# Value projection of one attention layer: two groups of eight heads with 512 columns per product, instead of four groups of four heads with 256

## The chip, the cores and the metric

The kernel runs on one core of a Trainium2 chip. The metric is the device time of one execution in microseconds (us). TensorE (PE) multiplies, VectorE (DVE) and ScalarE (ACT) do the elementwise work, GpSimd (POOL) does some elementwise work and issues a few transfers, and SyncE (SP) issues most transfers.

## The reference, cut to what matters

A trunk of two layers over 1024 positions and 1024 channels. Layer 0 has dilated attention and pooling side by side, layer 1 a gated unit and a state-space layer (S5); each layer ends with cross-attention. The change touches the attention of layer 0 alone:

```
hn = rms_norm(x, norm_ab[i])
z = hn @ w_in_ab[i]
q, k, v, g_a, v_b, g_b = jnp.split(z, [...], axis=-1)     # q, k, v: 1024 columns, 16 heads of 64
a_out = dilated_attention(q, k, v).reshape(b, s, A_WIDTH) * jax.nn.silu(g_a)
```

Each of three patterns (window, dilation) is a banded softmax over keys at a stride; the three are mixed by their denominators.

## The kernel before, in words

Every product of f32 matrices is made of three passes over rounded halves (high times high, high times low, low times high), so a product with 1024 input channels is 8 x 3 = 24 matmuls into one PSUM tile. The weights come in tiles of 128x1024 in a fixed list (`plan`). `get` loads tiles ahead through the SP queue (`wst`), ACT copies the rounded high half (`wh`, L177) and DVE subtracts for the low half (`wl`, L178); `s.deep` says how many are loaded and split ahead.

The stage of interest (`ab_main` with `ab_side`) handles the 16 heads as eight pairs, `pr` = 0 to 7. For each pair, `ab_pair` projects q, k and the gate (`ga`): three weights times two halves of the positions, six tiles of 24 matmuls with 512 columns, line L203 to L205. The values of several heads are projected ahead of them by `ab_v`: for each of eight blocks of 128 positions (`tt`) a tile with the positions on the partitions, which ACT scales (`vt`, L464) and writes to a scratch tensor in HBM; `ab_pair` reads its two heads' columns from there (`V`, `Vp`).

The attention itself is a second generator, `ab_side`. It works in 64 blocks, numbered here i = 8 x pair + b. A step of it is: the transposes of block i-1 (`turn`, PE L547 and L551), the scores of block i (`front`, PE L519), the products of block i-1 with the values (`mix`, PE L566), and every fourth step the products of the strided keys (`last`, PE L577). Between `front` of a block and its transposes lies the softmax for two heads: DVE adds the mask (L526) and takes the maximum (L527), ACT exponentiates (L528), DVE inverts the sum and scales (L529, L530). After the transposes ACT copies a part out of PSUM (`PT`, L553), which `mix` reads, and DVE another (`PTr`, L556). "Turn i" below means the transposes of block i on PE.

`drive` interleaves the two: whenever the main generator yields 1, the side generator earns 0.55 of a step. `mm3` with 8 terms yields once in its middle, and `ab_pair` once after each tile. `in_order` fixes PE's order to the order of the program text, so between two attention steps stand as many products as the yields let through. A pair may start only when the attention is at most two pairs behind:

```
            while s.attn_done < pr - 2:
                yield 2
```

A yield of 2 runs one step of the side at once, with no product between. From its eighth step on, each attention step also takes a piece of the S5 layer's preparation (`s5_prep`, mostly small POOL operations, L904 to L909, on tiles `s5z` and `trig`) and places it behind the step's own instructions.

Of the kernel before, what the change touches and what calls it, by code (L numbers as in the profile page):

```python
# [10 lines left out]
AF = mybir.ActivationFunctionType  # L11
# [19 lines left out]
def layout(i):  # L31
    f = {n: np.asarray(v) for n, v in i.items()}
    c = np.ascontiguousarray
    o = {}
    o["xT"] = c(f["x"][0].T.reshape(8, 128, 1024))
    o["memT"] = c(f["mem"][0].T.reshape(8, 128, 256).transpose(1, 0, 2).reshape(128, 2048))
    cols = [f["norm_ab"][0], f["norm_cd"][0], f["norm_x"][0], f["norm_x"][1], f["mem_norm"], f["final_norm"],
            f["pool_scale"][0], f["sgu_ln_g"][0], f["sgu_ln_b"][0]]
    o["gains"] = c(np.stack(cols).reshape(72, 128).T)
    o["w_kv"] = c(np.stack([_chunks(f["w_xkv"][l]) for l in range(2)]))  # L40
    o["w_q"] = c(np.stack([_chunks(f["w_xq"][l].T) for l in range(2)]))
    o["w_o"] = c(f["w_xo"].reshape(2, 4, 2, 128, 2, 512).transpose(0, 1, 4, 3, 2, 5).reshape(2, 8, 128, 1024))
    w = f["w_in_ab"][0]
    o["w_ab"] = c(_chunks(np.concatenate([w[:, :2048], w[:, 3072:]], axis=1)))
    o["w_v"] = c(w[:, 2048:3072].reshape(2, 4, 128, 4, 256).transpose(3, 0, 2, 1, 4).reshape(8, 128, 1024))
    o["pool_w"] = c(f["pool_w"][0].reshape(4, 2, 128, 256).transpose(0, 2, 1, 3).reshape(4, 128, 512))
    o["w_out_ab"] = c(f["w_out_ab"][0].reshape(2, 8, 128, 8, 128).transpose(3, 0, 2, 1, 4).reshape(16, 128, 1024))
    w = f["w_in_cd"][0]
    o["w_cd"] = c(_chunks(np.concatenate([w[:, :1024], w[:, 2048:]], axis=1)))
    o["w_vc"] = c(w[:, 1024:2048].reshape(4, 2, 128, 2, 512).transpose(3, 0, 2, 1, 4).reshape(8, 128, 1024))  # L50
    o["w_glu"] = c(np.concatenate([_chunks(f["glu_w1"][0]), _chunks(f["glu_w2"][0])], axis=2))
    o["w_out_cd"] = c(f["w_out_cd"][0].reshape(2, 6, 128, 8, 128).transpose(3, 0, 2, 1, 4).reshape(16, 128, 768))
    o["sgu_wT"] = c(f["sgu_w"][0].transpose(2, 0, 1).reshape(128, 512))
    o["sgu_b"] = c(np.broadcast_to(f["sgu_b"][0].reshape(1, 512), (128, 512)))

    def both(t):
        rep = np.broadcast_to(t.T[None], (2, 64, 32)).reshape(128, 32)
        pair = t.reshape(16, 2, 64).transpose(1, 2, 0).reshape(128, 16)
        return np.concatenate([rep, pair], axis=1)

    dt = np.broadcast_to(f["s5_log_dt"][0][:, None], (32, 64))
    o["s5_p"] = c(np.concatenate([both(f["s5_a_re"][0]), both(f["s5_a_im"][0]), both(dt)], axis=1))
    st = []
    for n in ("s5_b_re", "s5_b_im"):
        st.append(f[n][0].transpose(1, 0, 2).reshape(64, 512))
    for n in ("s5_c_re", "s5_c_im"):
        st.append(f[n][0].transpose(2, 0, 1).reshape(64, 512))
    st = np.stack(st, axis=1).reshape(64, 2048)
    o["s5_bc"] = c(np.broadcast_to(st[None], (2, 64, 2048)).reshape(128, 2048))
    d = f["s5_d"][0].reshape(32, 16).T  # L70
    o["s5_d"] = c(np.broadcast_to(d[None], (8, 16, 32)).reshape(128, 32))

    p = np.arange(128)
    t = 4 * (p % 32) + p // 32
    j1 = np.concatenate([t, t + 128])
    dist = 128 + t[:, None] - j1[None, :]
    m1 = np.where((dist >= 0) & (dist <= 128), 0.0, NEG)

    def m23(q, k):
        dd = q[:, None] - k[None, :]  # L80
        n = (dd >= 0) * ((dd <= 128).astype(int) + (dd % 4 == 0))
        return np.where(n == 0, NEG, np.where(n == 2, math.log(2.0), 0.0))

    cst = [m23(p % 32, np.arange(32)), m1[:, 128:], m23(p % 32 + 224, np.arange(256)), m1]
    cst.append(np.eye(128, 240))
    cst.append(np.broadcast_to(1.0 / np.arange(1, 17)[None], (128, 16)))
    cst.append(((p[:, None] >= 112) & (p[:, None] % 16 == np.arange(16)[None])).astype(float))
    o["cst"] = c(np.concatenate(cst, axis=1).astype(np.float32))
    return o
# [6 lines left out]
class Prog:  # L96
    def __init__(s, nc, tc, a, pool, psum, dram):
        s.nc, s.tc, s.a, s.pool, s.psum, s.dram = nc, tc, a, pool, psum, dram
        s.plan, s.index, s.W, s.st = [], {}, {}, {}
        s.n_load = s.n_split = s.pos = 0  # L100
# [81 lines left out]
    def get(s, key):  # L182
# [7 lines left out]
        s.pos = i + 1  # L190
        return s.W[i]

# [256 lines left out]
            s.flush()  # L449
        s.last = p  # L450

    def ab_v(s, qd):
        nc = s.nc
        vd = s.dt(f"v{qd}", [1024, 256])
        s.vd[qd] = vd
        keys = [("v", 2 * qd), ("v", 2 * qd + 1)]
        W = [s.get(k) for k in keys]
        for tt in range(8):
            p = s.pm()
            h, o = tt // 4, 128 * (tt % 4)  # L460
            yield from s.mm3(p[:, :256], [((s.xg[k, h][0][:, o:o + 128], s.xg[k, h][1][:, o:o + 128]),
                                           tuple(w[:, 256 * (k % 4):256 * (k % 4) + 256] for w in W[k // 4])) for k in range(8)])
            t = s.u("vt")
            nc.scalar.activation(t[:, :256], p[:, :256], AF.Copy, scale=s.Rt[:, tt:tt + 1])  # L464
            nc.scalar.dma_start(vd[128 * tt:128 * tt + 128, :], t[:, :256])
        for k in keys:
            s.free(k)

    def ab_pair(s, pr):
        nc = s.nc  # L470
        q, kk, ga = (s.b(n) for n in ("q", "kk", "ga"))
        V, Vp = s.b("V"), s.b("Vp")
        vd, c0 = s.vd[pr // 2], 128 * (pr % 2)
        for r in range(4):
            nc.sync.dma_start(V[32 * r:32 * r + 32, :].rearrange("i (t c) -> i t c", t=8),
                              vd[:, c0:c0 + 128].rearrange("(t i r) c -> r i t c", i=32, r=4)[r])
        for hh in range(2):
            nc.sync.dma_start(Vp[:, 512 * hh:512 * hh + 512].rearrange("p (r c) -> p r c", r=4),
                                vd[512 * hh:512 * hh + 512, c0:c0 + 128].rearrange("(p r) c -> p r c", r=4))
        held, R8 = {}, s.R8  # L480
        for h in range(2):
            yield from s.proj(("ab", pr), h, held)
            s.anchor = nc.vector.tensor_tensor(q[:, 512 * h:512 * h + 512].rearrange("p (b r i) -> p b r i", b=4, r=4),
                                               s.last.rearrange("p (b i r) -> p b r i", b=4, r=4),
                                               R8[h].rearrange("p (b i r) -> p b r i", b=4, r=4), op=ALU.mult)
            yield 1
        for h in range(2):
            yield from s.proj(("ab", 8 + pr), h, held)
            s.anchor = nc.vector.tensor_tensor(kk[:, 512 * h:512 * h + 512].rearrange("p (b r i) -> p b r i", b=4, r=4),
                                               s.last.rearrange("p (b i r) -> p b r i", b=4, r=4),  # L490
                                               s.R[h].rearrange("p (b i r) -> p b r i", b=4, r=4), op=ALU.mult)
            yield 1
        for h in range(2):
            yield from s.proj(("ab", 16 + pr), h, held)
            s.anchor = nc.vector.tensor_tensor(ga[:, 512 * h:512 * h + 512], s.last, s.R[h], op=ALU.mult)
            if h == 1:
                nc.scalar.activation(ga, ga, AF.Silu)
            yield 1
        s.pair[pr] = (q, kk, ga, V, Vp)
# [148 lines left out]
    def ab_main(s):  # L648
        s.R8 = [s.u("R8") for _ in range(2)]
        for h in range(2):  # L650
            s.nc.gpsimd.tensor_scalar(s.R8[h], s.R[h], 0.125, None, op0=ALU.mult)
        s.vd, s.pair, s.gd, s.attn_done = {}, {}, {}, -1
        for pr in range(8):
            if pr % 2 == 0:
                yield from s.ab_v(pr // 2)
            while s.attn_done < pr - 2:
                yield 2
            yield from s.ab_pair(pr)
        for gi in range(4):
            if s.attn_done == 7:  # L660
                s.mtags = ("mm", "s", "o")
            yield from s.ab_pool(gi)
# [768 lines left out]
def plan(s):  # L1431
    a = s.a
# [8 lines left out]
        for d in range(8):  # L1441
            s.add(("o", l, d), a["w_o"][l, d])
    for pr in range(8):
        if pr % 2 == 0:
            s.add(("v", pr), a["w_v"][pr])
            s.add(("v", pr + 1), a["w_v"][pr + 1])
        for j in (0, 8, 16):
            s.add(("ab", j + pr), a["w_ab"][j + pr])
    for gi in range(4):
# [83 lines left out]
```

## Time and profile before

| | |
|---|---|
| time, median of 3 runs | 2112.68 us (2112.36 to 2113.53) |
| profiled execution | 2116.89 us, of which 2115.2 us span |
| mean granted TensorE clock | 0.989 |
| PE busy | 2061.8 us (97%) |
| DVE, ACT, POOL busy | 1144.8, 767.5, 534.8 us |

The span runs from the first to the last instruction of the program; busy times are unions of an engine's instructions. PE is the engine that nearly always works; the other three wait for it, or it for them in short places. The stage of the attention runs from 200 to about 850 us of the span.

### The profile page before, as it was taken

How to read it: one execution, taken by the hardware profiler on the slowest of the kernel's cores; microseconds unless marked ns; L12 is line 12 of the kernel's file. 1: busy time of each engine (PE TensorE's matmuls, PEld its weight loads, DVE VectorE, ACT ScalarE, POOL GpSimd, SP SyncE). 2: the span in 40 equal slices, each digit the busy share in tenths (PEclk: the TensorE clock that was granted, in tenths of full speed). 3: DMA queues.
4: the chain of work that ended last, by engine and by line, in shares of the span. 5: the costliest groups of instructions: out<-in, count | busy, mean ns of one | idle time of the engine just before them, and what ended most of it. 6: DMA issues, size and time to landing. Idle time of an engine off the chain costs nothing.

```text
span 2115.2 us, 33157 instructions
## 1 busy us (share of the span) xinstructions
PE 2061.8 (97%) x12974; PEld 1729.7 (82%) x12974; DVE 1144.8 (54%) x2067; ACT 767.5 (36%) x1442; POOL 534.8 (25%) x802
## 2 busy tenths in 40 slices
PE   8999999899999988999999999999999999999998
PEld 8999888687787766888888888888888887888887
DVE  6664266566655775456453655444653334555554
ACT  7765243333333333114332444212221122443453
POOL 4332017722333244122111003221221100220013
PEclk9999999999999999999999999999999999999999
DMA  7888212103114112116464125532331134642142
GB/s 293 301 292 281 73 33 86 56 24 119 51 65 114 62 51 86 56 66 222 146 208 164 46 101 183 166 119 70 116 113 70 58 102 157 202 165 74 51 169 80
DMA packets 131468, 258.63 MB, mean 122 GB/s; under 512 B 13040, under 2 KB 63344, under 8 KB 131312
## 3 DMA queue, kind: packets, MB, share of 16 engines
q1 hardware_dynamic: 86608, 189.39, 26.8%
q0 software_dynamic: 13440, 43.53, 5.6%
q10 hardware_dynamic: 31264, 23.60, 3.6%
q8 instruction: 102, 1.67, 0.3%
q14 instruction: 54, 0.44, 0.1%
HBM read 193.02 MB, written 63.44 MB: 121 GB/s over the span
## 4 chain that ended last, share of the span: by engine, by line
PE 87%; DVE 5%; POOL 3%; ACT 2%; issue 2%; DMA 1%; SPq 0%; DVEq 0%; ACTq 0%; POOLq 0%
PE ps_mm L203 13%; PE ps_mm L204 13%; PE ps_mm L205 13%; PE ps_s L204 5%; PE ps_s L205 5%; PE ps_s L203 5%; PE ps_o L205 4%; PE ps_o L204 4%; PE ps_o L203 4%; PE ps_s L519 2%; PE ps_o L566 1%; PE ps_mm L1311 1%; PE ps_mm L1309 1%; PE ps_mm L1310 1%; PE ps_t L547 1%
## 5 line engine op out<-in xcount | busy, mean ns | idle before, releaser
L178 DVE TENSOR_TENSOR wl<-wst,wh 128x1024 fp32r<-128x1024 f32 (+1 forms) x263 | 345.8, 1329 | 128.3 <-ACT wh L177 123.3
L203 PE MATMUL ps_mm<-xg,wh 128*128 128x512 f32 x880 | 350.1, 398 | 1.3 <-DVE ug L1338 1.0
L204 PE MATMUL ps_mm<-xg,wh 128*128 128x512 f32 x880 | 343.7, 391 | 0.0
L205 PE MATMUL ps_mm<-xg,wl 128*128 128x512 f32 x880 | 343.3, 390 | 0.0
L177 ACT ACTIVATE wh<-wst 128x1024 fp32r<-128x1024 f32 (+1 forms) x263 | 262.0, 1016 | 113.4 <-PE ps_mm L204 84.5
L203 PEld LDWEIGHTS ps_mm<-xg,wh 128*128 128x128 f32 x880 | 165.4, 188 | 43.3 <-issue 8.3
L205 PEld LDWEIGHTS ps_mm<-xg,wl 128*128 128x128 f32 x880 | 165.3, 188 | 34.9
L204 PEld LDWEIGHTS ps_mm<-xg,wh 128*128 128x128 f32 x880 | 165.6, 188 | 32.4 <-issue 0.2
L240 POOL TENSOR_TENSOR acc<-acc,sq 128x512 f32<-128x512 f32 (+1 forms) x81 | 102.5, 1266 | 215.0 <-ACT sq L236 202.5
L223 ACT ACTIVATE xg<-x,gains 128x512 fp32r<-128x512 f32 x64 | 46.2, 722 | 246.3 <-DVE x L753 187.4
L528 ACT ACTIVATE P<-P,mx 128x320 f32<-128x320 f32 (+7 forms) x128 | 77.9, 610 | 136.6 <-DVE mx L527 132.9
L553 ACT ACTIVATE PT<-ps_t 128x256 f32<-128x256 f32 (+1 forms) x128 | 45.3, 369 | 174.2 <-PE ps_t L551 172.7
L592 POOL DMA_DIRECT2D gab<-G x32 | 18.1, 567 | 244.2 <-DVE G L580 126.9
L530 DVE TENSOR_SCALAR P<-P,den 128x320 f32<-128x320 f32 (+7 forms) x128 | 77.2, 604 | 4.4
L556 DVE COPY PTr<-ps_t 128x128 f32<-128x128 f32 (+2 forms) x192 | 46.0, 281 | 55.8 <-ACT PT L553 52.8
L224 DVE SCALAR_TENSOR_TENSOR xg<-x,gains,xg 128x512 fp32r<-128x512 f32 x64 | 52.1, 815 | 42.1 <-ACT xg L223 40.8
L203 PE MATMUL ps_mm<-wh,xg 128*128 128x256 f32 x256 | 73.9, 289 | 0.0
L205 PE MATMUL ps_mm<-wh,xg 128*128 128x256 f32 x256 | 72.5, 283 | 0.0
L204 PE MATMUL ps_mm<-wl,xg 128*128 128x256 f32 x256 | 72.4, 283 | 0.0
L1338 DVE TENSOR_TENSOR ug<-ps_mm,R 128x512 f32<-128x512 f32 x32 | 22.1, 689 | 90.4 <-PE ps_mm L205 90.3
L526 DVE TENSOR_TENSOR P<-ps_s,cst 128x320 f32<-128x320 f32 (+7 forms) x128 | 65.0, 549 | 8.3 <-PE ps_s L519 6.4
L547 PE MATMUL ps_t<-cst,P 128*128 128x128 f32 x240 | 47.5, 281 | 21.0 <-DVE den L529 15.0
(423 smaller groups left out, 5115.1 us busy)
## 6 DMA issues: line engine op xcount, KB each, us to landing
wst<-w_ab SPq DMA_DIRECT2D x40, 512.0 KB, 3.4
wst<-w_out_ab SPq DMA_DIRECT2D x32, 512.0 KB, 4.3
wst<-vsc SPq DMA_DIRECT2D x32, 512.0 KB, 4.0
wst<-w_kv SPq DMA_DIRECT2D x31, 512.0 KB, 5.9
wst<-w_cd SPq DMA_DIRECT2D x24, 512.0 KB, 3.4
wst<-w_out_cd SPq DMA_DIRECT2D x32, 384.0 KB, 3.3
wst<-w_q SPq DMA_DIRECT2D x16, 512.0 KB, 8.1
msc<-mo ACTq DMA_DIRECT2D x32, 256.0 KB, 6.2
```

Of the source, the lines that this page charges most:

```text
L177: s.last_hi = s.nc.scalar.activation(H[:, :w], t[:, :w], AF.Copy)
L178: s.nc.vector.tensor_tensor(L[:, :w], t[:, :w], H[:, :w], op=ALU.subtract)
L203: s.nc.tensor.matmul(ps, lhsT=lh, rhs=rh, start=(i == 0), stop=False)
L204: s.nc.tensor.matmul(ps, lhsT=lh, rhs=rl, start=False, stop=False)
L205: s.nc.tensor.matmul(ps, lhsT=ll, rhs=rh, start=False, stop=(i == n - 1))
L223: nc.scalar.activation(H, x, AF.Copy, scale=g)
L224: nc.vector.scalar_tensor_tensor(L, x, g, H, op0=ALU.mult, op1=ALU.subtract)
L240: nc.gpsimd.tensor_tensor(st["acc"][:, :n], st["acc"][:, :n], q[:, :n], op=ALU.add)
L526: nc.vector.tensor_tensor(t[:, :n], p[e][:, :n], s.cst[:, m0:m0 + n], op=ALU.add)
L528: j = nc.scalar.activation(t[:, :n], t[:, :n], AF.Exp, bias=mx, accum_out=den)
L530: nc.vector.tensor_scalar(t[:, :n], t[:, :n], den, None, op0=ALU.mult)
L547: nc.tensor.transpose(pt[:, 128 * j:128 * j + 128], t[:, n2 + 128 * j:n2 + 128 * j + 128], s.ident)
```

## The change

The 1024 value columns are projected in two groups (`g`) instead of four (`qd`). A product has 512 columns instead of 256, and a group reads four weight tiles, which are taken one by one as the first block of positions needs them and given back one by one in the last. Within a group, five tiles instead of three are split ahead. `ab_v` yields twice per block of positions instead of once. `ab_main` calls it before pairs 0 and 4 instead of before pairs 0, 2, 4 and 6, and the list of weights follows.

```
-    def ab_v(s, qd):
-        nc = s.nc
-        vd = s.dt(f"v{qd}", [1024, 256])
-        s.vd[qd] = vd
-        keys = [("v", 2 * qd), ("v", 2 * qd + 1)]
-        W = [s.get(k) for k in keys]
+    def ab_v(s, g):
+
+        nc = s.nc
+        s.vd[g] = vd = s.dt(f"v{g}", [1024, 512])
+        keys = [("v", 4 * g + j) for j in range(4)]
+        W, deep = {}, s.deep
+        s.deep = (1, 5)
         for tt in range(8):
             p = s.pm()
             h, o = tt // 4, 128 * (tt % 4)
-            yield from s.mm3(p[:, :256], [((s.xg[k, h][0][:, o:o + 128], s.xg[k, h][1][:, o:o + 128]),
-                                           tuple(w[:, 256 * (k % 4):256 * (k % 4) + 256] for w in W[k // 4])) for k in range(8)])
+            for k in range(8):
+                if k // 2 not in W:
+                    W[k // 2] = s.get(keys[k // 2])
+                H, L = W[k // 2]
+                c0 = 512 * (k % 2)
...
+                nc.tensor.matmul(p, lhsT=lh, rhs=H[:, c0:c0 + 512], start=(k == 0), stop=False)
+                nc.tensor.matmul(p, lhsT=lh, rhs=L[:, c0:c0 + 512], start=False, stop=False)
+                nc.tensor.matmul(p, lhsT=ll, rhs=H[:, c0:c0 + 512], start=False, stop=(k == 7))
+                if tt == 7 and k % 2 == 1:
+                    if k == 7:
+                        s.deep = deep
+                    s.free(keys[k // 2])
+                if k == 3:
+                    yield 1
             t = s.u("vt")
-            nc.scalar.activation(t[:, :256], p[:, :256], AF.Copy, scale=s.Rt[:, tt:tt + 1])
-            nc.scalar.dma_start(vd[128 * tt:128 * tt + 128, :], t[:, :256])
-        for k in keys:
-            s.free(k)
+            nc.scalar.activation(t, p, AF.Copy, scale=s.Rt[:, tt:tt + 1])
+            nc.scalar.dma_start(vd[128 * tt:128 * tt + 128, :], t)
+            yield 1
...
         for pr in range(8):
-            if pr % 2 == 0:
-                yield from s.ab_v(pr // 2)
+            if pr % 4 == 0:
+                yield from s.ab_v(pr // 4)
             while s.attn_done < pr - 2:
                 yield 2
             yield from s.ab_pair(pr)
```

What PE does between two attention steps changes with it. First the place at the start of pair 2, from turn 5 on. The names are those of the section above; `ps_o<-PT,V` is `mix`, `ps_t<-cst,P` the transposes, `ps_s<-kk,q` a `front`. Before, `mix` of block 5 was followed by 48 products of the second value group, of which the first three stand here:

```order
L547 MATMUL ps_t<-cst,P 128x128 x2
L551 MATMUL ps_t<-cst,P 128x128 x2
L519 MATMUL ps_s<-kk,q 32x256 x8
L519 MATMUL ps_s<-kk,q 32x224 x8
L566 MATMUL ps_o<-PT,V 64x4x32 x4
L203 MATMUL ps_mm<-wh,xg_648 128x256
L204 MATMUL ps_mm<-wl,xg_648 128x256
L205 MATMUL ps_mm<-wh,xg_648 128x256
```

Now the same `mix` is followed by turn 6, `front` of block 7, `mix` of block 6 and turn 7 (the lines are 14 higher in the new text):

```order
L533 MATMUL ps_s<-kk,q 32x256 x8
L533 MATMUL ps_s<-kk,q 32x224 x8
L580 MATMUL ps_o<-PT,V 64x4x32 x4
L561 MATMUL ps_t<-cst,P 128x128 x2
L565 MATMUL ps_t<-cst,P 128x128 x2
L561 MATMUL ps_t<-cst,P 128x128 x2
L565 MATMUL ps_t<-cst,P 128x128 x2
L533 MATMUL ps_s<-kk,q 32x256 x16
L580 MATMUL ps_o<-PT,V 64x4x32 x4
L561 MATMUL ps_t<-cst,P 128x128 x2
L565 MATMUL ps_t<-cst,P 128x128 x2
```

The products between `front` and turn of a block, counted through PE's whole order, change like this (24 products are one tile; a number with "v" is of the value projection, with 256 columns before and 512 now):

| turn | 5 | 6 | 7 | 8 | 14 | 15 | 16 | 31 | 32 | 39 | 40 | 46 | 47 | 48 |
|---|---|---|---|---|---|---|---|---|---|---|---|---|---|---|
| before | 12+12v | 48v | 48v | 48v | 24 | 24 | 0 | 72 | 0 | 12+12v | 48v | 24 | 72 | 0 |
| now | 12 | 0 | 0 | 0 | 12 | 12 | 0 | 144+24v | 0 | 12 | 0 | 12 | 12 | 0 |

Turns 23 to 31 run beside the second value group (before: 23 to 28 beside the third of four, half as wide). Turns 9, 10 and 41 to 45 have 24 products of the pairs and none of the value projection, of which they had some before. Turns 49 to 63 are as before.

Second, DVE's order at the end of pair 2. `s5z` is the S5 preparation, whose RECIPROCAL waits for POOL. Before, it stood behind block 15's softmax and ahead of block 16's:

```order
L529 RECIPROCAL den<-den 128x1
L530 TENSOR_SCALAR P<-P,den 128x512
L495 TENSOR_TENSOR ga<-ps_mm,R_81 128x512
L556 COPY PTr<-ps_t 128x4x32 x2
L1028 RECIPROCAL s5z<-s5z 128x48
L526 TENSOR_TENSOR P<-ps_s,cst 128x160 x2
```

Now it stands inside block 15's softmax (128x512), ahead of its scaling:

```order
L540 TENSOR_TENSOR P<-ps_s,cst 128x512 x2
L541 TENSOR_REDUCE mx<-P 128x1 x2
L1042 RECIPROCAL s5z<-s5z 128x48
L543 RECIPROCAL den<-den 128x1
L544 TENSOR_SCALAR P<-P,den 128x512
L509 TENSOR_TENSOR ga<-ps_mm,R_81 128x512
```

On POOL, 113 instructions now stand between the transfer of block 7's result (`gab<-G`) and the one that this RECIPROCAL waits for, instead of 120; the other seven have moved ahead of the transfer.

## Rows read from the trace of the kernel before

**Rows 1.** The chain that ended last, from the page: share of the span by engine.

```profile
PE 87%; DVE 5%; POOL 3%; ACT 2%; issue 2%; DMA 1%; SPq 0%; DVEq 0%; ACTq 0%; POOLq 0%
```

**Rows 2.** Windows: stretch, length, PE, PEld, DVE, ACT, POOL busy, PEclk, DMA.

```profile
223.00:985.00 762.00, 731.24 (x6038) 592.15 (x6037) 452.58 (x951) 244.59 (x526) 274.13 (x519) 0.98 0.22 71
```

**Rows 3.** Lines L203 and L519: count, shortest/median/longest ns, first and last start.

```profile
L203 PE MATMUL ps_mm<-xg,wh x880: 387/389/796, 223.4 to 1736.1; 128*128 128x512 f32 x176
...
L203 PE MATMUL ps_mm<-wh,xg x256: 277/283/388, 200.3 to 633.8; 128*128 128x256 f32 x128
...
L519 PE MATMUL ps_s<-kk,q x2048: 189/376/633, 261.6 to 817.6; 64*32 64x256 f32 x94, 64*32 64x128 f32 x23, 64*32 64x64 f32 x12, 64*32 64x160 f32 x12
```

**Rows 4.** Timeline of PE, turn 10 to turn 11: start, duration, instruction.

```profile
343.76 0.38 PE L547 MATMUL ps_t<-cst,P 128*128 128x128 f32 x2
...
345.90 0.50 PE L203 MATMUL ps_mm<-xg,wh 128*128 128x512 f32 x1
...
351.48 0.38 PE L547 MATMUL ps_t<-cst,P 128*128 128x128 f32 x2
```

**Rows 5.** Timeline of PE, turn 22; [idle before <- what ended it].

```profile
445.83 0.41 PE L547 MATMUL ps_t<-cst,P 128*128 128x128 f32 x2 [0.63 <-DVE P L530]
```

**Rows 6.** Timeline of all engines, turn 15 to turn 16.

```profile
385.61 0.38 PE L547 MATMUL ps_t<-cst,P 128*128 128x128 f32 x2
...
386.65 1.28 ACT L497 ACT_TABLE_LOAD   x1
...
387.94 1.06 ACT L497 ACTIVATE ga<-ga 128x1024 f32<-128x1024 f32 x1
...
389.33 0.65 PE L566 MATMUL ps_o<-PT,V 128*64 128x128 f32 x6 [1.88 <-ACT PT L553]
...
392.01 0.45 DVE L1028 RECIPROCAL s5z<-s5z 128x48 f32<-128x48 f32 x1 [4.86 <-POOL s5z L909]
...
395.69 0.45 PE L547 MATMUL ps_t<-cst,P 128*128 128x128 f32 x1 [5.71 <-DVE den L529]
```

**Rows 7.** Timeline of DVE and ACT, softmax of block 6.

```profile
304.62 0.98 DVE L556 COPY PTr<-ps_t 128x128 f32<-128x128 f32 x4 [1.60 <-ACT PT L553]
...
305.67 1.22 DVE L526 TENSOR_TENSOR P<-ps_s,cst 128x480 f32<-128x480 f32 x2
...
306.81 1.20 DVE L527 TENSOR_REDUCE mx<-P 128x1 f32<-128x480 f32 x2
...
307.53 1.28 ACT L528 ACT_TABLE_LOAD   x1 [2.44 <-DVE mx L527]
...
308.82 0.70 ACT L528 ACTIVATE P<-P,mx 128x480 f32<-128x480 f32 x1
...
309.84 0.47 DVE L530 TENSOR_SCALAR P<-P,den 128x480 f32<-128x480 f32 x1
```

**Rows 8.** Timeline of PE, turns 8, 32 and 48 and the product behind each.

```profile
328.35 0.27 PE L547 MATMUL ps_t<-cst,P 128*128 128x128 f32 x1
...
331.69 0.39 PE L203 MATMUL ps_mm<-wh,xg 128*128 128x256 f32 x1
...
536.78 0.65 PE L566 MATMUL ps_o<-PT,V 128*64 128x128 f32 x6 [1.88 <-ACT PT L553]
539.24 0.45 PE L547 MATMUL ps_t<-cst,P 128*128 128x128 f32 x1 [1.81 <-DVE den L529]
...
545.51 0.50 PE L203 MATMUL ps_mm<-xg,wh 128*128 128x512 f32 x1
...
685.00 0.30 PE L547 MATMUL ps_t<-cst,P 128*128 128x128 f32 x1 [1.81 <-DVE den L529]
...
690.09 0.50 PE L203 MATMUL ps_mm<-xg,wh 128*128 128x512 f32 x1
```

**Rows 9.** Windows, the step that begins with turn 32; columns as in group 2.

```profile
540.00:546.00 6.00, 6.00 (x72) 4.82 (x71) 3.64 (x11) 1.69 (x6) 0.00 (x0) 0.55 0.01 3
```

**Rows 10.** Timeline of POOL: the transfer of block 7's result.

```profile
333.25 0.64 POOL L592 DMA_DIRECT2D gab<-G  x1 [3.76 <-DVE den L529]
```

More of the change, by code (lines that the diff above doesn't have):

```diff
@@ L44, in layout @@
     o["w_ab"] = c(_chunks(np.concatenate([w[:, :2048], w[:, 3072:]], axis=1)))
-    o["w_v"] = c(w[:, 2048:3072].reshape(2, 4, 128, 4, 256).transpose(3, 0, 2, 1, 4).reshape(8, 128, 1024))
+    o["w_v"] = c(w[:, 2048:3072].reshape(4, 2, 128, 2, 512).transpose(3, 0, 2, 1, 4).reshape(8, 128, 1024))
     o["pool_w"] = c(f["pool_w"][0].reshape(4, 2, 128, 256).transpose(0, 2, 1, 3).reshape(4, 128, 512))
@@ L460, in ab_v @@
             h, o = tt // 4, 128 * (tt % 4)
-            yield from s.mm3(p[:, :256], [((s.xg[k, h][0][:, o:o + 128], s.xg[k, h][1][:, o:o + 128]),
-                                           tuple(w[:, 256 * (k % 4):256 * (k % 4) + 256] for w in W[k // 4])) for k in range(8)])
+            for k in range(8):
[3 more added lines that the diff above has]
+                c0 = 512 * (k % 2)
+                xh, xl = s.xg[k, h]
+                lh, ll = xh[:, o:o + 128], xl[:, o:o + 128]
+                nc.tensor.matmul(p, lhsT=lh, rhs=H[:, c0:c0 + 512], start=(k == 0), stop=False)
[7 more added lines that the diff above has]
+                    yield 1
             t = s.u("vt")
-            nc.scalar.activation(t[:, :256], p[:, :256], AF.Copy, scale=s.Rt[:, tt:tt + 1])
-            nc.scalar.dma_start(vd[128 * tt:128 * tt + 128, :], t[:, :256])
-        for k in keys:
-            s.free(k)
+            nc.scalar.activation(t, p, AF.Copy, scale=s.Rt[:, tt:tt + 1])
+            nc.scalar.dma_start(vd[128 * tt:128 * tt + 128, :], t)
+            yield 1
     def ab_pair(s, pr):
@@ L472, in ab_pair @@
         V, Vp = s.b("V"), s.b("Vp")
-        vd, c0 = s.vd[pr // 2], 128 * (pr % 2)
+        vd, c0 = s.vd[pr // 4], 128 * (pr % 4)
         for r in range(4):
@@ L1443, in plan @@
     for pr in range(8):
-        if pr % 2 == 0:
-            s.add(("v", pr), a["w_v"][pr])
-            s.add(("v", pr + 1), a["w_v"][pr + 1])
+        if pr % 4 == 0:
+            for j in range(4):
+                s.add(("v", pr + j), a["w_v"][pr + j])
         for j in (0, 8, 16):
```

## The prediction

> **What bounds the kernel now.** I read the chain that ended last first: PE holds 87% of it [rows 1], so a change is worth what it takes from PE's work, less the new holes that it opens in it. The change lies in the attention stage, so I then read the windows: PE works 731.2 of 762 us there [rows 2]. The holes, 31 us, are few, and what ends them is the softmax (DVE, ACT) or the copy behind the transposes (ACT), seen in the timeline. An attention step is a loop over four engines, and PE can go on only because products stand between `front` of a block and its turn. With 24 of them, turn 11 follows turn 10 after 7.72 us without a wait; the step's own PE work is 345.90 - 343.76 = 2.1 us of it [rows 4]. With 12, turn 22 waits 0.63 us [rows 5]. With none, PE stands: 1.88 us for the copy and 1.81 us for the softmax around turn 32 [rows 8], 1.88 and 5.71 us around turn 16 [rows 6]. So cover is what to count, and the order of instructions gives it exactly.
>
> **What is removed.** The first value group begins at 200.3 us and the first projection behind it at 223.4, so 192 products of 256 columns take 23.1 us, 0.120 us each; the 168 products of 512 columns from 223.4 to the first `front` at 261.6 take 0.227 us each [rows 3]. 768 x 0.120 = 92.4 us become 384 x 0.227 = 87.3 us: **-5.1 us**, and it all lies on PE's path. The Trainium skill (TensorE: Matmul & The Clock Gate, Back-to-back issue gap) puts a warm product at N / 2.4 GHz plus 2.5 ns, which is 109 and 216 ns; by it the gain would be 1.0 us, and the sum below 4 us higher. The evictions (`vt`) and their transfers halve in number; ACT is not what PE waits for there, so I cost them at nothing, covered by the products of the next block of positions.
>
> **What is moved: cover.** The products of two value groups used to stand beside turns 5 to 10 and 39 to 44. They now stand ahead of pair 0, where no attention runs, and beside turns 23 to 31, which were covered anyway. As pair 2 and later pair 3, 6 and 7 must not start before the attention has caught up, side steps are now run in a row.
>
> *Turns 6, 7, 8* lose 48 products each.
> - Turn 6 comes just after pair 1's gate. As in turn 15 to 16, ACT loads a table and runs the SiLU between the two copies out of PSUM, so that `mix` goes on only 389.33 - 385.61 = 3.72 us after the turn's start [rows 6]. Behind it stand two `PTr` copies, two mask additions, the first maximum, a second table load that itself waits for the maximum, the exponential and the scaling; in block 6 that was 304.62 to 310.31, 5.69 us with four copies, so 5.2 with two [rows 7]. Together 8.9 us, against own PE work of about 2.5 (2.1 in rows 4 for a small block; these are larger, an estimate): 6.4 us lost. From below: the 3.4 of turn 7; from above: turn 16's 7.6 plus the clock, 10.5 [rows 6].
> - Turn 7 has no table load. With 12 products the hole is 0.63 us [rows 5]; without these 2.73 us more: 3.4.
> - Turn 8 is the small first block of the next pair, like turn 32: 1.88 + 1.81 = 3.7 [rows 8].
> - The clock: from turn 8 to the next product PE took 3.34 us where nothing had stopped it, and 6.27 us from turn 32, behind two idle stretches [rows 8], with a granted clock of 0.55 in that window, that is mostly 1.2 instead of 2.4 GHz [rows 9]. I add the 2.9 us once.
>
> Together **+16.4** (10.2 to 34).
>
> The Trainium skill (ScalarE: Activation LUTs, What ACT_TABLE_LOAD costs) adds a drain of 1.38 us to each load of 1.28. Here the SiLU starts 1.29 us after its load [rows 6] and the exponential 1.29 us after its own [rows 7], so I see no drain; with it, turns 6 and 40 would cost 2.8 us more each.
>
> *Turns 14 and 15* keep 12 of 24 products: 2 x 0.63 = **+1.3** (0 to 3.8, the second by 1.88 each).
>
> *Turns 15 and 16 and POOL.* DVE's RECIPROCAL of the S5 preparation waited 4.86 us for POOL already [rows 6], and held turn 16. It now stands in front of block 15's scaling, so it holds turn 15. POOL's time to it hangs on the transfer of block 7's result, which came 333.25 - 328.35 = 4.9 us after turn 8 [rows 8, 10]; with the slow clock 7.8. From there to the RECIPROCAL at 392.01 were 58.8 us for 120 instructions, now 113: 55.3. So turn 15 can start at turn 8 plus 63.1, plus the RECIPROCALs and the scaling, 64.3. PE itself would be there after 6.3 + 5.5 to turn 9, 4 x 7.72 + 1.0 (one `last`) to turn 13 and 2 x 5.6 for the half-covered ones, 55 us; such steps were sometimes a little longer, so I take a stall of 8 instead of 9.5. Turn 16 then costs what turn 32 did, 3.7 + 2.9 = 6.6, instead of 7.6 + 2.9 = 10.5. Net **+4.1** (-3.9 if POOL is in time, +6).
>
> *Turns 39, 46, 47* are left with 12 products: 3 x 0.63 = 1.9. *Turn 40* has none: 6.6 like turn 32. *Turn 48* had none before either, but 72 products just ahead; it cost 3.7 + (5.09 - 3.34 = 1.75) [rows 8] and now 6.6: 1.2. Together **+9.7** (3.7 to 17).
>
> Turn 31 gets 168 products in a row; attention is starved there, PE is not. The weights of the value groups are split among other work: for the first group in the prologue, ahead of 200 us, for the second at turns 18 to 22, so I cost this at nothing; the cover is one attention step per tile.
>
> **Sum**: -5.1 + 16.4 + 1.3 + 4.1 + 9.7 = +26.4 us. On the profiled execution's 2116.9 us that is 2143.3; this execution was 4.2 us above the median of the runs, 2112.7, so the time to expect is **2139 us**. The low ends add to -5.1 + 10.2 + 0 - 3.9 + 3.7 = +4.9 (2118), the high ones to some +56 (2169).
>
> **Rivals.**
> 1. *The chain shrinks to nothing* (other side). In steps that run in a row, DVE and ACT have no q, k or gate to evict and few weights to split, so softmax might follow at once; then only the 5.1 us are left: 2107.6 us. It decides at turn 6: the gain wins if all new holes stay under 5.1 us. Against it: around turn 32 nothing else ran on DVE or ACT than the step itself and the table loads, and PE still stood 3.7 us [rows 8]. Chance 0.05.
> 2. *POOL is in time* (turn 15). If it needs under 47 us for its 113 instructions, turn 15 waits for the softmax alone, and -3.9 takes the place of +4.1: +18, 2131; with turn 6 at 3.4 as well, 2128. For it: the 58.8 us may hold waits of POOL for other engines, which then go. Against it: DVE waited 4.86 us for POOL with more time given [rows 6]. Chance 0.22.
> 3. *A table load costs twice.* If ACT must run empty ahead of each load, its 1.28 us [rows 6, 7] count double where nothing covers them, at turns 6 and 40 with two loads each: 5.1 us more, 2144. Against it the 1.29 us above. The Trainium skill's drain, named above, is this case. Chance 0.03.
> 4. *Weights come late* in the second group: ACT's rounding of a tile stands ahead of a block's exponential, and if its transfer has not landed, the whole loop waits. Two holes like that of turn 16, 5.7 us [rows 6], give +11: 2150. Against it: the order has most loads there a turn or more ahead of their rounding, and every rounding ahead of the tile's first product by several. Chance 0.07.
> 5. *Cheap holes*: everything near its low end, 2113 to 2121, within or just over no change. Chance 0.05.
>
> **How the numbers follow.** The forecast, +20 to +40 us, has 0.55; the rest of 0.03 is above it. The range from 2122 to 2156 takes in rivals 2, 3 and 4 and the forecast with its unknown stall of turns 6 and 15, and leaves out rivals 1 and 5 and some of the upper tail. About 0.2% (4.2 us) is what a measurement of this kernel tells from no change. Faster needs rival 1, 0.05; same 0.04, most of rival 5; slower 0.91.
>
> **What would show it.** PE's busy time falls by the products removed, while its idle time in the stage grows from 31 to about 55 us. Turn 6 should wait 4 us or more for DVE behind a wait of `mix` for ACT; turns 7, 8 and 40 near 3 to 4; the RECIPROCAL of `s5z` should wait for POOL with turn 15 behind it; granted clock below 1 in three or four more places. Wrong would be: turns 6 to 8 follow within 4 us of each other, or PE waits for weights.

## The result, and the profile after

| | before | after |
|---|---|---|
| median of 4 runs | 2113.11 us (2112.36 to 2114.30) | 2138.78 us (2137.16 to 2141.59) |
| profiled execution, its span | 2116.89, 2115.2 us | 2137.69, 2136.0 us |
| mean granted TensorE clock | 0.989 | 0.985 |

After is 1.0122 times before (95% interval 1.0105 to 1.0140), 25.7 us slower by the medians and 20.8 us by the two profiled executions. The lines below are of the profile after; 14 is to be added to the line numbers of the kernel before. "Half clock" is a granted clock of 0.5, that is 1.2 instead of 2.4 GHz.

The chain that ended last, share of the span by engine, as in [rows 1]:

```profile
PE 89%; DVE 6%; POOL 2%; ACT 2%; issue 1%; DMA 0%; SPq 0%; DVEq 0%; ACTq 0%; POOLq 0%
```

Windows (stretch, length, PE, PEld, DVE, ACT, POOL busy, PEclk, DMA): the attention stage as in [rows 2], longer by the span's growth, and the stretches around turns 6 to 8.

```profile
223.00:1006.00 783.00, 733.96 (x5740) 579.22 (x5739) 449.49 (x947) 238.24 (x509) 271.23 (x518) 0.97 0.22 69
...
320.00:330.00 10.00, 4.83 (x57) 3.32 (x55) 5.66 (x15) 6.18 (x12) 6.13 (x19) 0.86 0.68 194
330.00:340.00 10.00, 6.13 (x57) 4.23 (x58) 6.93 (x17) 4.13 (x10) 6.65 (x18) 0.67 0.00 0
340.00:350.00 10.00, 8.84 (x119) 6.98 (x119) 6.74 (x24) 3.07 (x11) 5.74 (x19) 0.61 0.16 54
```

PE idles 49 us in the stage, 31 before [rows 2]: 18 of the 21 us. The other 3 are busy time, which rose from 731.2 to 734.0 us although fewer products are done: by the granted clock that the two traces record, between 200 and 870 us, half clock covers 54.5 us in eight stretches after and 34.1 us in six before. From 320 to 350 us PE works only two thirds of the time, and the mean clock falls to 0.6.

The two kinds of product, from the view of one line (count, shortest/median/longest ns, first and last start):

```profile
L469 PE MATMUL ps_mm<-wh,xg x128: 389/389/504, 200.1 to 535.5; 128*128 128x512 f32 x128
L203 PE MATMUL ps_mm<-xg,wh x880: 388/389/796, 243.6 to 1757.4; 128*128 128x512 f32 x176
```

From the first value product at 200.1 us to the first projection at 243.6 lie 192 products: 43.5 us, 0.227 us each. Twice that is 87.0 us, against 4 x 23.1 = 92.4 before [rows 3]: -5.4 us (predicted -5.1).

Timeline, from turn 5 to turn 8 (start, duration, engine, instruction, idle before it and what ended it):

```profile
322.85 1.28 ACT L511 ACT_TABLE_LOAD   x1
...
324.14 1.06 ACT L511 ACTIVATE ga<-ga 128x1024 f32<-128x1024 f32 x1
...
325.53 0.65 PE L580 MATMUL ps_o<-PT,V 128*64 128x128 f32 x6 [1.34 <-ACT PT L567]
...
327.75 1.28 ACT L542 ACT_TABLE_LOAD   x1 [2.28 <-DVE mx L541]
329.05 0.69 ACT L542 ACTIVATE P<-P,mx 128x480 f32<-128x480 f32 x1
...
330.68 0.66 PE L561 MATMUL ps_t<-cst,P 128*128 128x128 f32 x2 [4.51 <-DVE P L544]
...
338.13 0.66 PE L561 MATMUL ps_t<-cst,P 128*128 128x128 f32 x2 [3.18 <-DVE P L544]
...
342.99 0.45 PE L561 MATMUL ps_t<-cst,P 128*128 128x128 f32 x1 [1.16 <-DVE den L543]
```

The two table loads stand where they were expected, and PE waits 1.34 + 4.51 us around turn 6, 3.18 ahead of turn 7 and 1.16 ahead of turn 8. A pair of transposes of turn 6 is recorded with 0.66 us where turn 10 had 0.38 [rows 4]: half clock, as the windows show.

Turns 15 and 16:

```profile
402.80 0.45 DVE L1042 RECIPROCAL s5z<-s5z 128x48 f32<-128x48 f32 x1 [3.02 <-POOL s5z L923]
...
403.94 0.41 PE L561 MATMUL ps_t<-cst,P 128*128 128x128 f32 x2 [3.19 <-DVE P L544]
...
409.97 0.45 PE L561 MATMUL ps_t<-cst,P 128*128 128x128 f32 x1 [2.44 <-DVE den L543]
```

Turns 40 and 48, the second with what held it:

```profile
638.98 0.30 PE L561 MATMUL ps_t<-cst,P 128*128 128x128 f32 x1 [1.86 <-DVE den L543]
...
701.90 2.02 POOL L923 TENSOR_TENSOR s5w<-s5o,yz 128x1024 f32<-128x1024 f32 x1
702.43 1.59 DVE L544 TENSOR_SCALAR P<-P,den 128x160 f32<-128x160 f32 x1
...
704.17 0.45 PE L561 MATMUL ps_t<-cst,P 128*128 128x128 f32 x1 [4.49 <-DVE den L543]
```

**A ledger by turns.** Starts of turns 10, 17, 49 and 63 after, then of 17, 49 and 63 before (turn 10 is in [rows 4]).

```profile
361.81 0.38 PE L561 MATMUL ps_t<-cst,P 128*128 128x128 f32 x2
...
421.74 0.38 PE L561 MATMUL ps_t<-cst,P 128*128 128x128 f32 x2
...
715.63 0.38 PE L561 MATMUL ps_t<-cst,P 128*128 128x128 f32 x2
...
845.74 0.38 PE L561 MATMUL ps_t<-cst,P 128*128 128x128 f32 x2
```

```profile
407.58 0.38 PE L547 MATMUL ps_t<-cst,P 128*128 128x128 f32 x2
...
695.67 0.38 PE L547 MATMUL ps_t<-cst,P 128*128 128x128 f32 x2
...
824.48 0.41 PE L547 MATMUL ps_t<-cst,P 128*128 128x128 f32 x2 [0.23 <-DVE P L530]
```

From the difference of two starts the difference of the products done until then is taken away (counted in the order of instructions, at the prices above), and what is left was lost in holes or to the clock. "Lost" below is always this reckoning.

| until turn | 10 | 17 | 49 | 63 |
|---|---|---|---|---|
| later than before, us | 18.05 | 14.16 | 19.96 | 21.26 |
| of it products | +2.7 | -2.7 | -5.4 | -5.4 |
| lost | 15.3 | 16.9 | 25.4 | 26.7 |
| lost, as predicted | 16.4 | 21.8 | 31.5 | 31.5 |

### The profile page after: what moved, and what is told of

Same layout as the page of the kernel before. It is cut to its first block, busy times and chain, and to the rows that moved or that the text cites. A ratio compares the mean times of both kernels' runs of the same rounds, so it can differ in the third digit from the quotient of the medians.

```text
span 2136.0 us, 32323 instructions
## 1 busy us (share of the span) xinstructions
PE 2064.3 (97%) x12590; PEld 1713.0 (80%) x12590; DVE 1147.2 (54%) x2067; ACT 764.5 (36%) x1426; POOL 533.5 (25%) x802
## 4 chain that ended last, share of the span: by engine, by line
PE 89%; DVE 6%; POOL 2%; ACT 2%; issue 1%; DMA 0%; SPq 0%; DVEq 0%; ACTq 0%; POOLq 0%
PE ps_mm L203 12%; PE ps_mm L204 12%; PE ps_mm L205 12%; PE ps_s L204 5%; PE ps_s L205 5%; PE ps_s L203 5%; PE ps_o L204 4%; PE ps_o L205 4%; PE ps_o L203 4%; PE ps_s L533 2%; DVE P L544 1%; PE ps_mm L469 1%; PE ps_mm L1325 1%; PE ps_mm L471 1%; PE ps_mm L1324 1%; PE ps_mm L1323 1%
## 5 line engine op out<-in xcount | busy, mean ns | idle before, releaser
L203 PE MATMUL ps_mm<-xg,wh 128*128 128x512 f32 x880 | 350.4, 398 | 1.3 <-DVE ug L1352 1.0
L203 PEld LDWEIGHTS ps_mm<-xg,wh 128*128 128x128 f32 x880 | 165.5, 188 | 43.6 <-issue 8.6
L561 PEld LDWEIGHTS ps_t<-cst,P 128*128 128x128 f32 x240 | 31.2, 147 | 58.0 <-issue 43.7
L497 DVE TENSOR_TENSOR q<-ps_mm,R 128x512 f32<-128x512 f32 x16 | 17.7, 1104 | 102.8 <-PE ps_mm L205 102.8
L204 PE MATMUL ps_s<-gr,wh 128*128 128x512 f32 x168 | 65.9, 392 | 2.0 <-DVE gr L211 2.0
```

What stands on the lines that cost most here:

```text
L203: s.nc.tensor.matmul(ps, lhsT=lh, rhs=rh, start=(i == 0), stop=False)
L204: s.nc.tensor.matmul(ps, lhsT=lh, rhs=rl, start=False, stop=False)
L561: nc.tensor.transpose(pt[:, 128 * j:128 * j + 128], t[:, n2 + 128 * j:n2 + 128 * j + 128], s.ident)
```

## The experiments

The theory is that of the prediction: PE loses where no products stand between `front` and turn. Its rivals are named with each run. All ratios are to the kernel before, measured beside it. The profiled executions are compared turn by turn with the one of after or before.

**1. The old products in the new places.** The kernel before, whose value groups are moved; the list of weights follows.

```
-            if pr % 2 == 0:
+            if pr % 4 == 0:
                 yield from s.ab_v(pr // 2)
+                yield from s.ab_v(pr // 2 + 1)
```

> The value products keep 256 columns and the old two-tile groups, but two groups stand before pair 0 and two before pair 4, so the covers of turns 6 to 22 are those of the changed kernel (none at 6, 7, 8 and 16). Theory (the loss is the missing cover, the products give 5.1 us back): the changed kernel's 2138.8 us plus the 5.1 us that narrow products cost, 2144 us (2139 to 2149), with waits ahead of turns 6 and 7 of 3 to 5 us each. Rival (the loss comes with the form of the new products, their four weight tiles or the deeper split, not with their place): about 2113 us, and no more wait ahead of turns 6 and 7 than in the kernel before.

Measured: 2148.16 us, ratio 1.0158 (1.0145 to 1.0172), 33.9 us above before. In its timeline turns 6, 7 and 8 wait as in the profile after (4.51, 3.18, 1.16):

```profile
334.65 0.66 PE L547 MATMUL ps_t<-cst,P 128*128 128x128 f32 x2 [4.50 <-DVE P L530]
...
342.23 0.66 PE L547 MATMUL ps_t<-cst,P 128*128 128x128 f32 x2 [3.16 <-DVE P L530]
...
347.15 0.30 PE L547 MATMUL ps_t<-cst,P 128*128 128x128 f32 x1 [1.48 <-DVE den L529]
```

So the place alone makes the loss; wide products, larger weight groups and deeper splitting aren't needed for it: until turn 17 this kernel has lost 16.6 us, the changed one 16.9. Against the changed kernel's 25.7 us it is 8 us more, where 5 were expected for the products. The trace shows a hole of another kind that can account for the rest. Between turns 27 and 28, in the first tile of the fourth value group, PE waits 0.78 us for ACT's rounding of a weight tile and 3.91 us for DVE's subtraction, and half clock follows:

```profile
510.95 0.58 PE L204 MATMUL ps_mm<-wl,xg 128*128 128x256 f32 x1 [3.91 <-DVE wl L178]
```

**2. The new products, the second group back at turns 5 to 13.** The list of weights follows again.

```
-            if pr % 4 == 0:
-                yield from s.ab_v(pr // 4)
+            if pr in (0, 2):
+                yield from s.ab_v(pr // 2)
```

> The 512-column products and four-tile groups of the changed kernel, but the second group stands before pair 2 instead of pair 4, so turns 6 to 13 have value products as cover again, turn 24 loses its cover and turns 39 to 48 stay as in the changed kernel. Theory (place decides): 2113.1 less 5.1 for the products is 2108, plus about 5 us for the new hole at turn 24 and about 8 us for the one at turn 40, 2121 us (2113 to 2128), no wait over 1 us ahead of turns 6, 7 and 8. Rival (form decides: four tiles split while the attention runs): 2135 us or more, with PE waiting for weights inside the second group.

Measured: 2122.35 us, ratio 1.0038 (1.0026 to 1.0050). In the timeline turns 6, 7 and 8 no longer wait:

```profile
333.70 0.38 PE L561 MATMUL ps_t<-cst,P 128*128 128x128 f32 x2
...
341.86 0.38 PE L561 MATMUL ps_t<-cst,P 128*128 128x128 f32 x2
```

From 200 to 420 us PE idles 1.6 us in all (19.4 in the profile after), so the weights of a group of four tiles are not late even beside the attention. Bare turns 16 (1.8 us of wait), 24 (3.2), 32 (1.6), 40 (1.9) and 48 (4.6) are left. Together with the first run this settles that it is the place.

**3. The bare steps of pair 2 spread over pair 1.** `drive` asks a function for its rate.

```
             while s.attn_done < pr - 2:
                 yield 2
+            s.rate = 0.8 if pr == 1 else 0.55
             yield from s.ab_pair(pr)
```

> The changed kernel, with the side generator earning 0.8 instead of 0.55 of a step per yield while pair 1 is projected, so the steps that stood bare at the start of pair 2 are spread: turns 1, 2, 4, 5, 6 have 12 products, turns 3 and 7 have 24, turn 8 none. The work is the same. Theory (the 15 us lost before turn 10 are uncovered softmaxes): five half covers at about 0.8 us each and one bare turn at about 3 us are left, 7 of the 15 us, so 2131 us (2126 to 2135). Rival (the time before turn 10 is lost for another reason, such as weights or the first pair's start): 2139 us, unchanged.

Measured: 2136.63 us, ratio 1.0105 (1.0092 to 1.0118): a smaller gain than expected, above the range, and hardly under the changed kernel's 1.0122. Until turn 10 the step did half of what was hoped: it starts 4.1 us earlier than after (357.71 for 361.81), with 6.9 us of holes between 280 us and turn 10 for 10.2. Thin places were dearer than 0.8 us: 0.68 us in turn 0, which has 12 products here too, 1.15 in turn 4 and 1.40 in turn 6; around bare turn 8 it was 1.87 and 1.81. The rest was given back where nothing had been edited: turn 16 waits 6.55 us for 2.44, and turn 49 comes only 0.2 us earlier than after. What holds turn 16 is POOL. The RECIPROCAL of the S5 preparation has moved behind turn 15's copies, ahead of block 16's softmax:

```profile
404.03 0.45 DVE L1043 RECIPROCAL s5z<-s5z 128x48 f32<-128x48 f32 x1 [3.07 <-POOL s5z L924]
```

So a gain at one place shifts the steps that follow against POOL's work, and can be lost there.

**4. Products that nobody reads, in the bare steps of pair 2.**

```
                 yield 2
+                if pr == 2:
+                    p = s.pm()
+                    for j in range(12):
+                        H, L = s.xg[j % 8, 0]
+                        s.nc.tensor.matmul(p, lhsT=H[:, :128], rhs=H, start=(j == 0), stop=(j == 11))
```

> The changed kernel with 12 more 512-column products, read by nobody, behind each attention step that the start of pair 2 forces; each of turns 6 to 9 gets 12 of them, 48 in all, 10.9 us of added PE work. Nothing is left out. Theory (PE idles 10.2 us ahead of turns 6 to 8, and runs at half clock after it for about another 5 us): the idle time falls by about 8 us, the clock stays up and gives about 5 us back, in sum 2137 us (2133 to 2141), and no granted clock under 0.9 between 325 and 350 us. Rival (the clock falls for another reason than these idle places): about 2142 us, with the clock still at 0.5 there. Second rival (the idle time was no waiting for the softmax): the 10.9 us are simply added, 2150 us.

Measured: 2136.05 us, ratio 1.0102 (1.0089 to 1.0115). Work was added and no time: turn 10 starts 0.5 us earlier than after (361.29). The waits ahead of turns 6 and 7 shrink:

```profile
330.63 0.41 PE L561 MATMUL ps_t<-cst,P 128*128 128x128 f32 x2 [1.56 <-DVE P L544]
...
336.81 0.41 PE L561 MATMUL ps_t<-cst,P 128*128 128x128 f32 x2 [0.31 <-DVE den L543]
```

The windows of the three stretches, whose clock was 0.86, 0.67 and 0.61 in the profile after:

```profile
320.00:330.00 10.00, 7.72 (x69) 5.45 (x67) 5.63 (x15) 6.19 (x12) 5.45 (x16) 1.00 0.72 194
330.00:340.00 10.00, 9.01 (x112) 6.44 (x113) 8.34 (x23) 4.45 (x11) 7.25 (x18) 1.00 0.02 5
340.00:350.00 10.00, 10.00 (x103) 8.20 (x102) 5.09 (x18) 2.63 (x10) 4.00 (x13) 1.00 0.20 77
```

10.9 us came in, the holes of turns 6 to 8 fell from 10.2 to 3.2 us, and the sum is -0.5: the half clock had cost 10.9 - 7.0 + 0.5 = 4.4 us there. It came from PE's idling, since it went with it. Further on the RECIPROCAL has moved as in the third experiment: it waits 5.29 us for POOL, and turn 16 waits 7.38.

**5. A pause for POOL.**

```
-            if n > 6 and n < 64:
+            if n > 6 and n < 64 and not 11 < n < 17:
```

> The changed kernel, with no piece of the S5 preparation taken at attention steps 12 to 16; POOL catches up, and the RECIPROCAL that waited for it moves from block 15's softmax to a block of pair 2 with 24 products before its turn. The work is the same. In the changed kernel PE waits 1.57 us at turn 14, 3.76 at 15 and 2.44 at 16. Theory (at turn 15 it is POOL that is late, at 14 and 16 the block's own softmax): turn 15 falls to about 1 us and turn 16 to 1.8, turn 14 stays, 3.4 us of idle time and 1 or 2 us of half clock are saved, 2134 us (2131 to 2137). Rival (the wait at turn 15 is the thin cover alone): 2139 us, unchanged.

Measured: 2132.62 us (2127.20 to 2140.15), ratio 1.0086 (1.0067 to 1.0105), within the expected range. Timeline of turns 15 and 16:

```profile
398.91 0.41 PE L561 MATMUL ps_t<-cst,P 128*128 128x128 f32 x2 [0.20 <-DVE P L544]
...
400.18 0.41 PE L561 MATMUL ps_t<-cst,P 128*128 128x128 f32 x2 [0.64 <-DVE P L544]
...
406.37 0.30 PE L561 MATMUL ps_t<-cst,P 128*128 128x128 f32 x1 [4.00 <-DVE den L543]
```

The wait of 3.19 + 0.57 us at turn 15 is 0.84 now, so it was POOL's. Turn 16 took some of it: 4.00 us for 2.44, against the expected 1.8. The block's first scaling takes 1.10 us there instead of 0.30, and ACT's first copy for `mix` comes 2.1 us after turn 15's start instead of 1.5. Turns 13 to 17 gain 3.0 us. Another 1.7 us stand ahead of turn 13, where nothing was edited: ahead of turn 9 the clock came back sooner, for no reason that the runs show (the last section has another such case). Of the 4.7 us together 1.2 are left at turn 49, since the moved pieces meet other turns (3.1 us of wait at turn 39 for 0.7), and 3.5 at turn 63. That the time met the expectation is in part luck; that turn 15's wait was POOL's is not.

**6 and 7. No bare turn at all,** for the wide products (in the places of the second experiment) and for the kernel before. In both:

```
     def ab_pair(s, pr):
+        held, R8 = {}, s.R8
+        yield from s.proj(("ab", pr), 0, held)
+        while s.attn_done < pr - 2:
+            yield 2
...
-            while s.attn_done < pr - 2:
-                yield 2
             yield from s.ab_pair(pr)
...
-        drive(tc, s.ab_main(), s.ab_side(), 0.55, -500)
+        drive(tc, s.ab_main(), s.ab_side(), 0.59, -500)
```

> The changed kernel with the second group before pair 2, the rate of the side generator 0.59 instead of 0.55, and the wait for the attention moved behind the first tile of a pair's products, so that no turn of the 64 is without at least 12 products before it. The work is the same. Theory (cover is all): from the 2122.4 us of the second experiment the bare turns 16, 24, 32, 40 and 48 go, with 1.8, 3.2, 1.6, 1.9 and 4.6 us of wait plus 1.9 us ahead of the products with the values each, 22 us in sum, of which the half covers that take their place keep about 8; 2108 us, and with their share of the half clock 2104 (2097 to 2112). Rival (the attention's own chain sets the pace at these places, whatever stands between): 2120 us or more.

> The kernel before (256-column products, four groups before pairs 0, 2, 4 and 6), with the same rate of 0.59 and the same later wait, so that no turn is bare here either. Theory (512-column products are worth their 5.1 us wherever the covers are alike): the bare turns 16, 32 and 48 of before, 5.7, 1.8 and 1.8 us and 1.9 us each ahead of the products with the values, 15 us, less about 5 for half covers, 2103 us (2097 to 2109), and within 4 us of the wide kernel in the same batch, which has two more thin places but 5.1 us less work; each of the two is faster than the kernel before. Rival (the wide form costs something of its own beside the attention): this one is 5 us or more faster than the wide one.

Measured: 2120.53 us, ratio 1.0027 (1.0016 to 1.0037), and 2122.49 us, ratio 1.0039 (1.0027 to 1.0051). Both expectations failed: all turns have 12 products or more, and the kernel before even became slower. Up to turn 49, with 12 products (2.7 us) more done by then, the first stands 1.4 us ahead of before and the second 0.7 behind; the thin places (1.7 and 3.0 us of wait at turn 23, 2.7 at 55) cost much of what the bare ones had. Then, in turn 61, ahead of the transposes of its second head, the timeline of the sixth kernel has this (the expectation of the tenth experiment calls it turn 62; the 448 columns are those of block 61):

```profile
797.22 0.56 DVE L548 TENSOR_SCALAR P<-P,den 128x448 f32<-128x448 f32 x1
...
798.20 13.38 DVE L548 TENSOR_SCALAR P<-P,den 128x448 f32<-128x448 f32 x1
...
810.08 1.25 POOL L925 TENSOR_TENSOR Ei<-s5w,s5w 128x512 f32<-128x512 f32 x1
811.73 0.66 PE L565 MATMUL ps_t<-cst,P 128*128 128x128 f32 x2 [11.47 <-DVE P L548]
```

A scaling that takes 0.44 us as a median runs for 13.38 us, and ends when POOL's row of TENSOR_TENSORs ends. The seventh kernel has the same step of 13.38 us, and 11.58 us of wait. Such steps stand in the other kernels too: 8 of the 128 scalings of the kernel before take 1.7 us or more (6.80 us at 744.29, which ends in turn 55's wait of 3.79), each beside TENSOR_TENSORs of POOL, some beside its MEMSETs as well, and so do 8 of after, with 1.59 us at turn 48 besides.

**8 to 11. The scaling on ACT,** for after, before and the two kernels of 6 and 7, one edit:

```
-                nc.vector.tensor_scalar(t[:, :n], t[:, :n], den, None, op0=ALU.mult)
+                nc.scalar.activation(t[:, :n], t[:, :n], AF.Copy, scale=den)
```

> The changed kernel with the softmax's last step, the scaling of P by the inverse sum, on ACT instead of DVE (same work). In the runs so far that DVE step takes 0.44 us as a median, but 1.6 to 13.4 us where it starts beside a chain of POOL's TENSOR_TENSORs, and ends when POOL lets go. Theory (DVE's scaling and POOL exclude each other, but this is only a small part of the changed kernel's loss): the waits at turn 48 (4.49 us) falls to about 2, those at 55 (3.79) and 62 (3.10) to under 1.5, about 8 us gained; ACT's step is some 0.25 us longer with its hop, twice at each of seven bare turns and less at the thin ones, 5 us lost; 2136 us (2129 to 2141), still over 20 us above the kernel before with the same edit. Rival (the change lost its time by this exclusion): 2120 us or less.

> The kernel before with the same edit. Theory: the waits at turns 55 (3.79 us), 60 (1.86) and 62 (1.89) shrink, about 6 us gained, 3 lost at the bare and thin turns: 2110 us (2105 to 2116). Rival (the long DVE steps are a matter of the record and hold nobody up): 2116 us or more.

> The kernel of the sixth experiment (wide products, second group before pair 2, rate 0.59, later wait) with the same edit; there a single scaling step took 13.38 us, and PE waited 11.47 us for it at turn 62, which gave back all that the kernel had gained until then. Theory: that wait goes, with some 3 us of half clock behind it and about 4 us of the waits at turns 55 to 60, less 4 for the longer step: 2106 us (2099 to 2112). Rival (the attention's own chain holds PE there): 2118 us or more.

> The kernel of the seventh experiment (narrow products as before, rate 0.59, later wait) with the same edit; there the long step was 13.38 us too, with 11.58 us of wait. Theory: 2108 us (2101 to 2115), and the wide kernel of the same batch is 0 to 5 us faster, for its 5.1 us of cheaper products less two more thin places. Rival (wide products cost beside the attention): the narrow one is faster by 3 us or more.

| kernel | us | ratio (95%) |
|---|---|---|
| 8: after | 2132.23 | 1.0080 (1.0068 to 1.0093) |
| 9: before | 2111.91 | 0.9985 (0.9976 to 0.9993) |
| 10: wide, no bare turn | 2099.96 | 0.9924 (0.9910 to 0.9937) |
| 11: narrow, no bare turn | 2099.91 | 0.9923 (0.9909 to 0.9936) |

In the timeline of the tenth kernel turn 61 goes on beside the same row on POOL, without a wait (turn 62 then waits 0.69 us):

```profile
792.87 0.66 ACT L548 ACTIVATE P<-P,den 128x448 f32<-128x448 f32 x1
...
794.15 0.38 PE L565 MATMUL ps_t<-cst,P 128*128 128x128 f32 x2
```

In the eighth kernel the waits at turn 55 (0.49 us for 3.79) and 62 (none for 3.10) went as well. Of that at turn 48 (1.27 for 4.49) most only moved: turn 47 waits 2.99 us there for 0.94.

The rival for the change falls: with the exclusion gone from both, after is still 20.3 us above before. What the edit is worth depends on where POOL happens to meet the attention: 3 us for before, 7 to 9 for after, 21 to 25 for the two kernels that had met it worst (by medians, and by ratios).

Kernels 10 and 11 beat before by 15 to 16 us (by medians, and by ratios). The expectation for the eleventh failed twice: it is faster than its range, and the wide kernel is not the faster of the two. The wide one lost 6.8 us more until turn 13, at turn 5, ahead of its second value group: 1.5 + 2.3 us of wait, and 6.8 us at half clock behind them. From there on the two lose alike.

```profile
322.37 1.04 ACT L177 ACTIVATE wh<-wst 128x1024 fp32r<-128x1024 f32 x1
...
324.68 0.44 PE L565 MATMUL ps_t<-cst,P 128*128 128x128 f32 x2 [1.51 <-ACT P L548]
...
327.60 0.69 PE L565 MATMUL ps_t<-cst,P 128*128 128x128 f32 x2 [2.27 <-ACT P L548]
```

It isn't the cover: turn 5 has 12 products in both kernels, and in the narrow one it waits only 1.2 us, ahead of `mix`. But in the wide one two weight tiles are split between turns 4 and 5, and the rounding above stands between block 5's two exponentials; in the narrow one none is. The sixth and seventh kernels differ alike (2.4 us ahead of turn 5 and none). So the 5.4 us of products were gained, and spent at one place, where weights are split inside a softmax. No run changes that alone; it is read from the traces.

## Why the prediction was right, step by step

**The time** (2139 predicted, 2138.78 measured) is better than its sum. Profile against profile the sum said +26.4 and the two executions differ by 20.8; the forecast then took off 4.2 us, because the profiled execution of before was slow against its median, while that of after was 1.1 us fast. That the errors met is luck, and the measured ratio leaves 22 to 30 us open anyway; the sign and the order of size are not luck.

**Products**: -5.4 for -5.1. The Trainium skill's formula (TensorE: Matmul & The Clock Gate, Back-to-back issue gap), which the page gives for a product by itself, would have given -1.0; the rows of both widths (0.120 and 0.227 us, with a new weight load ahead of each product) decide against it. PE's busy time did not fall by the products, as "What would show it" said, but rose by 2.7 us in the stage: half clock took back more than they gave. It came in two more stretches, not in three or four, but in longer ones.

**Turns 6, 7, 8**: +16.4 predicted, 15.3 lost until turn 10. The parts were off in both directions: turn 6 idles 5.85 us (6.4 lost was predicted), turn 7 3.18 (3.4), turn 8 1.16 (3.7), and the half clock cost 4.4 by the fourth experiment (2.9). Turn 8 was priced like turn 32, and that counted 1.88 us twice. At turn 32 they are the wait of `mix` for the copy, which a table load and the SiLU hold up, as at turn 15 [rows 6]. Here these stand at turn 5, where the sum for turn 6 had them already, and `mix` of block 7 does not wait. What is left, 1.16 us for 1.81, may be the clock: at half clock PE's own work in the step is longer (0.79 us for the 32 products of `front`, 0.51 ahead of turn 40), and the softmax runs beside it. Experiments 1 and 2 show the cause, the place of the groups.

**The table loads** cost what the rows said: 324.14 - 322.85 and 329.05 - 327.75 are 1.29 and 1.30 us from load to use, so rival 3 and the drain of the Trainium skill (ScalarE: Activation LUTs, What ACT_TABLE_LOAD costs) don't show here.

**Turns 14 to 16** is the term that was mis-sized: +1.3 and +4.1 predicted, 16.9 - 15.3 = 1.6 measured. The mechanism was right, the RECIPROCAL waited for POOL and turn 15 for it, as the fifth experiment confirms; but it waited 3.02 us and the turn 3.76, not 8. POOL needed 402.80 - 342.99 = 59.8 us from turn 8 instead of 63.1 (6.7 us to the transfer for 7.8, and 53.1 behind it for 55.3), and PE came 2.8 us later than reckoned. Each was a small error, and the stall is the difference of two long times. So rival 2 was near: POOL was neither in time nor 8 us late.

**Turns 17 to 49**: +9.7 predicted, 8.5 measured, for partly other reasons. Turn 40 cost less, 1.86 us with the clock at full speed, where 6.6 were predicted: neither the 1.88 us for the copy nor the 2.9 for the clock came. Turn 48 waits longer, 4.49 us where 3.7 were reckoned, and the scaling of 1.59 us that POOL held up is in it. That step was not in the sum. Neither was turn 22, which has its 12 products as before but waits 1.38 + 0.38 us for 0.63 [rows 5]: a weight tile of the second group is split between block 22's two maxima.

```profile
458.24 1.21 DVE L178 TENSOR_TENSOR wl<-wst,wh 128x1024 fp32r<-128x1024 f32 x1
...
460.74 0.41 PE L561 MATMUL ps_t<-cst,P 128*128 128x128 f32 x2 [1.38 <-DVE P L544]
```

So the splitting, which the prediction put at nothing, costs 1.1 us there.

**Weights** (rival 4) were not late: in the profile after no value product waits for ACT's rounding or DVE's subtraction, and in the second experiment neither. Rival 1, that steps in a row shrink to nothing, is refuted by 18 us more of idle time.

## What to carry to other kernels

Count the work that lies between the issue of a loop over several engines and its use, place by place: moving independent products away from such a place costs far more than cheaper products give back, here 26.7 us for 5.4. But a count of cover is no price: thin places cost from nothing to 3.0 us each here, and 12 products cover less when weights are split inside the softmax beside them, so judge such an edit by the holes of the trace and not by the number of bare places. When an elementwise instruction takes many times its median, look at what the engine beside it was doing in just that time before looking for a late input.

## What the runs showed of the hardware

A DVE TENSOR_SCALAR in SBUF, 128x448 in f32, took 13.38 us, where the one just before it took 0.56, beside an unbroken row of POOL TENSOR_TENSORs, and PE waited 11.47 us for it; with the same step on ACT the turn did not wait. The Trainium skill (SBUF — State Buffer, Who interferes with whom) says that DVE, in its modes that use two ports, and GpSimd share a pair of ports under an exclusive lock, held for a whole instruction. No run here shows in which mode the step ran. The trace agrees that one keeps the other out wholly, but DVE did not get in between POOL's instructions: it waited through a row of them, to 811.6 us, the end of the last one at 811.33 included.

The same hole cost differently with the clock. Windows that begin 1.2 us behind the start of turn 40, of after and then of the third experiment, where it stands 3 us earlier with the same instructions around it:

```profile
640.15:645.15 5.00, 5.00 (x76) 4.28 (x56) 3.61 (x10) 2.18 (x6) 0.50 (x1) 1.00 0.16 59
```

```profile
637.00:642.00 5.00, 5.00 (x70) 4.56 (x49) 3.71 (x10) 1.24 (x5) 0.00 (x0) 0.66 0.16 63
```

The wait ahead of the turn is 1.86 us in both, but the clock stays up in one and falls to half in the other, and there turn 41 follows after 10.8 us instead of 9.2. The price of one place in one trace is thus good to some 2 us only.
